# Where the weight rows lie in a partition: a row step of 576 bytes for the input weights, and the output weights moved to the address residue of the left factors

## The chip, the cores and the metric

The kernel runs on one core of one Trainium2 chip. The metric is device time in microseconds for one launch. Five engines matter here: TensorE (PE in the profile, with its weight loads as PEld), VectorE (DVE), ScalarE (ACT), GpSimd (POOL) and the queue of SyncE (SP), which issues nearly all transfers. All of them work on SBUF, a memory of 128 partitions; "address" below always means a byte offset inside a partition, the same for all partitions.

## The reference, cut to what matters

One layer over 528 rows (16 learned tokens and 512 inputs) of 2048 numbers:

```python
hn = _rmsnorm(h_res, norm_in_g[l])
P = hn @ w_in[l]                       # 2048 -> 8320 columns
...                                     # RWKV-7 recurrence on one half, gated short convolution on the other
mix = jnp.concatenate([y_a, y_b], axis=-1)
h_res = h_res + mix @ w_out[l]         # 2048 -> 2048
out = _rmsnorm(h_res, norm_f_g)[:, N_META:]
```

The result has to be accurate to fp32, so each product of two matrices is made of three: a number is split into a high part that the fast fp32 mode of TensorE (fp32r) holds exactly and a low part, and high times high, high times low and low times high are added up.

## The kernel before, in words

**Input projection.** The 8320 output columns are 65 tiles of 128 columns ("lora", and eight each of k, r, v, g, B, C, h and gc). One tile needs 16 blocks of 128 weight rows, and for each block the three products. The weights are the stationary operand of the matmul (TensorE loads 128x128 of them for each one), the normalised rows `xh`/`xl` stream past as the moving operand, in pieces of 264 columns (k, v, lora; two pieces), 258 and 256 (r, g, C, h) or 512 (B, gc). `steps` (line 305) issues these matmuls: 5472 in all. Its inner order is: high weights with `xh`, high weights with `xl`, low weights with `xh`, then the next block.

**How weights come in.** `prefetch` (line 128) loads half a tile (128x1024) into a raw buffer; `split_w` (line 121) cuts it into two quarters of 128x512 and writes the high part with ACT (line 124) and the low part with DVE or POOL (line 125). A quarter holds four blocks side by side, 512 bytes each. There are six buffers for high and six for low quarters. The first four tiles come in smaller pieces (`split_piece`, line 210).

**What sets the order.** PE's order is written out by hand: `fill` and `until` put the projection's matmuls between those of the recurrence. DVE, ACT and POOL are ordered by priorities, by hand in a few stretches. SP's queue is in order: a transfer that waits for a buffer holds the ones behind it.

**Output projection.** From 855 us on. Here the roles are turned: the left factors (`parts`, or the sums `sform` named S1, S3, S4, S5) are stationary and the output weights stream, 512 columns at a time. `product` (line 1213) issues 12 matmuls for a unit; there are 56 units (seven products of a Strassen-like scheme, four quarters of the inner dimension, two halves of the columns). `split_unit` (line 1184) splits output weights into the same twelve buffers as above, or, for the last four units, into the place of old left factors ("home", line 1281). Raw output weights come through `request`, `begin_chain` and `add_by_transfer`; the chain tiles `x..0` to `x..3` hold running sums of them. DVE adds finished products onto the residual rows (`onto`, line 1199), which `load_xa` (line 1262) and `load_xb` bring in; a list of calls by unit number (`at`, line 1259) sets when each is issued.

**Addresses.** A memory pool is a contiguous range of a partition, and its tiles lie one after the other, each rounded up to 32 bytes. In the program before, the twelve quarter buffers (2048 bytes each) start at 4128, the raw buffers follow, then at 40992 `xh`, `xl`, `rs`, `la`, `ones`, `omm`, `hv`, `smask` (pool `xp`), and from 118112 the small pool `tp` (`warm`, three buffers `tm` of 2304 bytes at 118144, 120448 and 122752, `var0`, two `pr`, `b0`, `cv`). After the input projection, `xp` and `tp` are closed and the pool `pw` takes their place from 40992: `ssq`, `fv`, sixteen S tiles of 4096 bytes, `xa0` to `xa3`, chain tile `x03` (at 123072 to 127168), `sh`, `sqj`. A tile of `pw` waits for the tiles that lay in its place (`reuse_waits="tile"`), and for no other.

Taken modulo 512 this means: every block of input weights, high or low, starts at 32. Row kt of `xh` and `xl` starts at 32 + 64 kt, since a row of x is 528 x 4 = 2112 bytes. All left factors start at 192, all output weights at 32, the home tiles at 192. "Distance" below is the address of the weights that are being loaded minus the address of the rows that stream meanwhile, modulo 512. In the input projection of before it goes down by 64 from one block to the next, so each tile goes through eight distances, or sixteen with both pieces of 264. In the output projection it is 192 - 32 = 160, and 0 for the four home units.

Of the kernel before, what the change touches and what calls it, by code (L numbers as in the profile page):

```python
# [18 lines left out]
P = 128  # L19
DM = 2048  # L20
KT = DM // P
SEQ = 512
META = 16
L = SEQ + META
CH = 64
NCH = SEQ // CH + 1
# [20 lines left out]


AHEAD, WEIGHTS = 6000, 3000


def _constants():
# [24 lines left out]
def hymba_kernel(ctx: ExitStack, tc: tile.TileContext, xt, xtok, front, w_in, w_out, pv, lup, cst, msk, gf, out):  # L77
    nc = tc.nc
# [3 lines left out]
    wp = ctx.enter_context(tc.tile_pool(name="wp", bufs=3))  # L82
# [22 lines left out]
    plan = [("lora", 0), ("k", 0), ("r", 0), ("B", 0), ("v", 0), ("k", 1), ("r", 1), ("v", 1), ("g", 0), ("g", 1)]  # L105
# [10 lines left out]
    N_IN = len(stream)  # L116
    stream += [w_out[0, g] for g in range(3)]
    quarters, chain, low = {}, {}, {}
    state = {"next": 0}

    def split_w(q, rq, eng):
        hi = wp.tile([P, 512], F32R, tag="hi", name=f"wh{q}", bufs=6)
        lo = wp.tile([P, 512], F32R, tag="lo", name=f"wl{q}", bufs=6)
        nc.scalar.copy(hi, rq)  # L124
        low[q] = eng.tensor_tensor(out=lo, in0=rq, in1=hi.bitcast(F32), op=ALU.subtract).ins  # L125
        quarters[q] = (hi, lo)
# [13 lines left out]
    cq = ph2.enter_context(tc.tile_pool(name="cq", bufs=1, side="right", reuse_waits="tile"))  # L140
    ph1 = ExitStack()
    xp = ph1.enter_context(tc.tile_pool(name="xp", bufs=1))
    xh = xp.tile([P, KT, L], F32R, name="xh")
    xl = xp.tile([P, KT, L], F32R, name="xl")
    rs = xp.tile([P, L], F32, name="rs")
    la = xp.tile([P, 2, L], F32R, name="la")
    ones = xp.tile([P, P + 2], F32R, name="ones")
    omm = xp.tile([P, 33], F32, name="omm")
    hv = xp.tile([P, 6, 8], F32, name="hv")
    hl = cp.tile([P, 2, 8], F32, name="hl")  # L150
    smask = xp.tile([P, NCH, CH], F32, name="smask")
# [6 lines left out]
    tp = ph1.enter_context(tc.tile_pool(name="tp", bufs=1))  # L158
# [49 lines left out]
        return t  # L208

    def split_piece(n, a, t):  # L210
        hi, lo = quarters[2 * n]
        cols = slice(a, a + t.shape[1])
        nc.scalar.copy(hi[:, cols], t)
        nc.vector.tensor_tensor(out=lo[:, cols], in0=t, in1=hi[:, cols].bitcast(F32), op=ALU.subtract)


    for n in range(4):
        quarters[2 * n] = tuple(
            wp.tile([P, 512], F32R, tag=tag, name=f"w{tag[0]}{2 * n}", bufs=6) for tag in ("hi", "lo")
        )  # L220
# [84 lines left out]
    def steps(ps, ranges, k4, q, ks=range(4), rs_=range(2)):  # L305
        hi, lo = quarters[q]
        for r, (a, b) in enumerate(ranges):
            if r not in rs_:
                continue
            for k in ks:  # L310
                kt = 4 * k4 + k
                w = slice(k * P, (k + 1) * P)
                for n, (ww, xx) in enumerate(((hi, xh), (hi, xl), (lo, xh))):
                    nc.tensor.matmul(  # L314
                        ps[r], ww[:, w], xx[:, kt, a:b], start=(kt == 0 and n == 0), stop=(kt == KT - 1 and n == 2)
                    )
                    yield (b - a) * 0.43

# [14 lines left out]
            nc.vector.tensor_tensor(out=dst[:, a - base : b - base], in0=p, in1=rs[:, a:b], op=ALU.mult)  # L333

    def shift_full(ps, m, name, dst):
        pr = tp.tile([P, L + 1], F32, tag="pr", name=f"pr_{name}", bufs=2)
        nc.gpsimd.memset(pr[:, 0:1], 0.0)
        scaled(FULL, ps, pr, -1)
        sh = tm(f"sh_{name}")[:, 0:L]
        nc.scalar.activation(sh, pr[:, 0:L], AF.Copy, scale=col(V_MU, m))  # L340
        for (a, b), d in dst:
            nc.vector.scalar_tensor_tensor(
                out=d, in0=pr[:, a + 1 : b + 1], scalar=omm[:, m : m + 1], in1=sh[:, a:b], op0=ALU.mult, op1=ALU.add
            )

    def shift_real(ps, m, name, dst):
        pr = tp.tile([P, L + 1], F32, tag="pr", name=f"pr_{name}", bufs=2)
# [112 lines left out]
    def mains():  # L460
        pa = banks(FULL, "lora", pm, "main")
        pb = banks(FULL, "k0", pz, "tz")
        pc = banks(TAIL, "r0", pm, "main")
        pd = [pi.tile([P, SEQ], F32, tag="ser", name="ps_B0")]
        four = ((pa, FULL), (pb, FULL), (pc, TAIL), (pd, REAL))
        for k in range(4):
            for n, (ps, rg) in enumerate(four):
                if k == n == 0:
                    hi, lo = quarters[0]
                    for ww, xx, first in ((hi, xh, True), (lo, xh, False), (hi, xl, False)):  # L470
                        for p, (a, b) in zip(ps, rg):
                            nc.tensor.matmul(p, ww[:, 0:P], xx[:, 0, a:b], start=first, stop=False)
                            yield (b - a) * 0.43
                    continue
                yield from steps(ps, rg, 0, 2 * n, (k,))
        for k4 in range(1, 4):
            for n, (ps, rg) in enumerate(four):
                h = 4 * (k4 // 2) + n
                if k4 == 2:
                    prefetch(h + 3)  # L480
                if (k4, n) == (3, 2):
                    yb = token_scale_sums()
                if (k4, n) == (3, 3):
                    yield from steps(ps, rg, k4, 2 * h + k4 % 2, range(2))
                    token_scale(yb, 4)
                    use("lora", 0, pa)
                    use("k", 0, pb)
                    yield from steps(ps, rg, k4, 2 * h + k4 % 2, range(2, 4))
                    continue
                for r in range(2 if n < 3 else 1):  # L490
                    if (k4, n, r) == (3, 2, 1):
                        token_scale(yb, 0)
                    yield from steps(ps, rg, k4, 2 * h + k4 % 2, range(4), (r,))
        use("r", 0, pc)
        use("B", 0, pd)
        for j in range(4, len(plan)):
# [100 lines left out]
    def behind(dst, src):  # L597
        with tc.issue_after(state["dma"]):
            nc.sync.dma_start(dst, src)
# [450 lines left out]
    pp = ctx.enter_context(tc.tile_pool(name="pp", bufs=1, side="right", reuse_waits="tile"))  # L1050
# [73 lines left out]
    pw = ctx.enter_context(tc.tile_pool(name="pw", bufs=1, reuse_waits="tile"))  # L1124
    po = ctx.enter_context(tc.tile_pool(name="po", bufs=8, space=PSUM, reuse_waits="tile"))
    ssq = pw.tile([P, 4, 5], F32, name="ssq")
    fv = pw.tile([P, 4, 3], F32, name="fv")
    sform = {
        (f, q): [pw.tile([P, 4, HT], F32R, tag=f"{f}{q}{a}", name=f"{f}{q}{a}") for a in range(2)]
        for q in range(2) for f in forms  # L1130
    }
    xa = [pw.tile([P, 1024], F32, name=f"xa{t}") for t in range(4)]

    def split_form(f, q):
        k, tk = forms[f]
# [13 lines left out]
    U = {unit: u for u, unit in enumerate(units)}  # L1149
# [34 lines left out]
    def split_unit(unit, t, home=None):  # L1184
        for q in range(2):
            rq = t()[:, q * 512 : (q + 1) * 512]
            if home is None:
                hi = wp.tile([P, 512], F32R, tag="hi", name=f"oh{U[unit]}{q}", bufs=6)
                lo = wp.tile([P, 512], F32R, tag="lo", name=f"ol{U[unit]}{q}", bufs=6)
            else:  # L1190
                hi, lo = home[q]
            nc.scalar.copy(hi, rq)
            nc.vector.tensor_tensor(out=lo, in0=rq, in1=hi.bitcast(F32), op=ALU.subtract)  # L1193
            right[unit, q] = (hi, lo)
# [64 lines left out]
    def at(u, fn, *args):  # L1259
        calls.setdefault(max(u, -1), []).append((fn, args))  # L1260

    def load_xa(t):
        behind(xa[t], xtok[t * P : (t + 1) * P, 0:1024])

    xb, gfs = [], []
# [32 lines left out]
    for half in range(2):  # L1298
        o = 28 * half
# [28 lines left out]
            at(n + 1, sums, 1)  # L1328
        at(6 + n, split_form, f, 1)
    for t in range(4):  # L1330
        at((0, 1, 8, 9)[t], load_xa, t)
    at(13, load_gain)
    for m in range(2):
        at(21 + m, load_xb, m)
# [161 lines left out]
```

## Time and profile before

| | |
|---|---|
| median of 3 runs | 1025.31 us (1024.43 to 1025.73) |
| span of the profiled execution, first to last instruction | 1023.6 us |
| TensorE busy, share of the span | 1006.6 us, 98% |
| VectorE / ScalarE / GpSimd busy | 686.1 / 393.8 / 273.8 us |
| granted TensorE clock, mean | 0.996 |

The profiled execution's own time is not given apart from its span; the median stands 1.7 us above the span. Times inside the run are microseconds from its first instruction. Matmuls are pipelined: a row's duration runs from its start to its modelled end and overlaps the next one, so the pace of TensorE is read from start to start, or from a piece of the chain of waits, which counts each stretch of time once.

### The profile page before, as it was taken

What the parts mean: (1) busy time and instruction counts of PE and PEld (TensorE: products, weight loads), DVE (VectorE), ACT (ScalarE), POOL (GpSimd) and SP (SyncE); (2) the same over time, 40 slices, a digit from 0 to 9 for tenths busy, and PEclk for the clock granted to TensorE, in tenths of its full rate; (3) what the DMA queues carried; (4) which work ended last, traced back from release to release, by engine and by line L of the source; (5) the groups of instructions that cost most, each with busy time, mean ns of one, the idle gap of its engine ahead of it and who ended that gap; (6) DMA issues with size and microseconds to landing.
All of it is one profiled execution on the core that took longest, in us unless ns stands there. A gap on an engine that the chain in (4) does not pass through costs nothing.

```text
span 1023.6 us, 23708 instructions
## 1 busy us (share of the span) xinstructions
PE 1006.6 (98%) x9723; PEld 919.0 (90%) x9723; DVE 686.1 (67%) x1239; ACT 393.8 (38%) x729; POOL 273.8 (27%) x292
## 2 busy tenths in 40 slices
PE   9999999999999999999999999999999999999996
PEld 8899998999988999998999998889889897787885
DVE  7677954587765569654669653244555697998787
ACT  7553423344313434322434322222222335445453
POOL 0122323233332323232322232123332332015001
PEclk9999999999999999999999999999999999999999
DMA  9526476546764364864263845867673688695754
GB/s 333 152 63 148 122 190 182 150 123 143 167 172 134 96 170 99 217 167 117 83 166 98 220 139 168 309 212 235 195 232 93 183 276 192 172 319 135 172 125 165
DMA packets 185036, 174.82 MB, mean 171 GB/s; under 512 B 121568, under 2 KB 142816, under 8 KB 184416
## 3 DMA queue, kind: packets, MB, share of 16 engines
q1 hardware_dynamic: 182336, 164.40, 55.8%
q0 software_dynamic: 2304, 8.39, 4.7%
q8 instruction: 76, 1.25, 0.5%
q10 hardware_dynamic: 288, 0.52, 0.1%
q14 instruction: 32, 0.26, 0.1%
HBM read 136.92 MB, written 36.35 MB: 169 GB/s over the span
## 4 chain that ended last, share of the span: by engine, by line
PE 68%; DVE 8%; DMA 4%; issue 2%; SPq 1%; ACT 1%; POOL 0%; DVEq 0%; ACTq 0%; POOLq 0%
PE ps_gc L314 8%; PE ps_h L314 8%; PE ps_B L314 7%; PE ps_k L314 7%; PE ps_v L314 7%; PE ps_C L314 7%; PE ps_g L314 7%; PE ps_r L314 7%; DVE ol L1193 3%; DMA wo<-in_w_out_dram 2%; PE M L1220 2%; PE g L659 1%; PE zs L984 1%; PE Q L1220 1%; DVE xb L1201 1%
## 5 line engine op out<-in xcount | busy, mean ns | idle before, releaser
L125 POOL TENSOR_TENSOR wl<-wr,wh 128x512 fp32r<-128x512 f32 x119 | 169.2, 1423 | 370.8 <-ACT wh L124 356.4
L124 ACT CAST wh<-wr 128x512 fp32r<-128x512 f32 x252 | 152.7, 618 | 294.8 <-PE ps_C L314 51.9
L125 DVE TENSOR_TENSOR wl<-wr,wh 128x512 fp32r<-128x512 f32 x133 | 100.9, 765 | 109.0 <-ACT wh L124 108.6
L314 PE MATMUL ps_k<-xh,wl 128*128 128x264 f32 x256 | 73.1, 286 | 1.1 <-DVE wl L125 1.1
L314 PE MATMUL ps_v<-xh,wh 128*128 128x264 f32 x256 | 73.0, 285 | 0.0
L314 PE MATMUL ps_h<-xh,wh 128*128 128x258 f32 (+1 forms) x256 | 72.8, 284 | 0.0
L314 PE MATMUL ps_k<-xh,wh 128*128 128x264 f32 x256 | 72.8, 284 | 0.0
L314 PE MATMUL ps_v<-xl,wh 128*128 128x264 f32 x256 | 72.7, 284 | 0.0
L314 PE MATMUL ps_v<-xh,wl 128*128 128x264 f32 x256 | 72.7, 284 | 0.0
L314 PE MATMUL ps_k<-xl,wh 128*128 128x264 f32 x256 | 72.6, 284 | 0.0
L314 PE MATMUL ps_C<-xh,wh 128*128 128x258 f32 (+1 forms) x256 | 72.6, 284 | 0.0
L314 PE MATMUL ps_h<-xh,wl 128*128 128x258 f32 (+1 forms) x256 | 72.3, 282 | 0.2 <-issue 0.2
L314 PE MATMUL ps_r<-xh,wh 128*128 128x258 f32 (+1 forms) x256 | 72.4, 283 | 0.0
L314 PE MATMUL ps_g<-xl,wh 128*128 128x258 f32 (+1 forms) x256 | 72.3, 282 | 0.0
L314 PE MATMUL ps_r<-xl,wh 128*128 128x258 f32 (+1 forms) x256 | 72.2, 282 | 0.0
L314 PE MATMUL ps_g<-xh,wl 128*128 128x258 f32 (+1 forms) x256 | 72.0, 281 | 0.0
L314 PE MATMUL ps_C<-xl,wh 128*128 128x258 f32 (+1 forms) x256 | 72.0, 281 | 0.0
L314 PE MATMUL ps_g<-xh,wh 128*128 128x258 f32 (+1 forms) x256 | 72.0, 281 | 0.0
L314 PE MATMUL ps_h<-xl,wh 128*128 128x258 f32 (+1 forms) x256 | 71.9, 281 | 0.0
L314 PE MATMUL ps_r<-xh,wl 128*128 128x258 f32 (+1 forms) x256 | 71.9, 281 | 0.0
L314 PE MATMUL ps_C<-xh,wl 128*128 128x258 f32 (+1 forms) x256 | 71.9, 281 | 0.0
L314 PE MATMUL ps_B<-xh,wl 128*128 128x512 f32 x128 | 51.3, 401 | 0.0
(353 smaller groups left out, 3006.2 us busy)
## 6 DMA issues: line engine op xcount, KB each, us to landing
wr<-in_w_in_dram SPq DMA_DIRECT2D x126, 512.0 KB
ct<-opd SPq DMA_DIRECT2D x64, 288.0 KB
wo<-in_w_out_dram SPq DMA_DIRECT2D x24, 512.0 KB
x<-in_w_out_dram POOLq DMA_DIRECT2D x16, 512.0 KB, 6.2
opd<-ar SPq DMA_DIRECT2D x8, 576.0 KB
opd<-gt SPq DMA_DIRECT2D x16, 288.0 KB
opd<-bt SPq DMA_DIRECT2D x64, 64.0 KB
x<-in_w_out_dram SPq DMA_DIRECT2D x8, 512.0 KB
```

The lines of the kernel that those rows point to most:

```text
L124: nc.scalar.copy(hi, rq)
L125: low[q] = eng.tensor_tensor(out=lo, in0=rq, in1=hi.bitcast(F32), op=ALU.subtract).ins
L314: nc.tensor.matmul(ps[r], ww[:, w], xx[:, kt, a:b], start=(kt == 0 and n == 0), stop=(kt == KT - 1 and n == 2))
L659: nc.tensor.matmul(z[h][:, c - c0], bk[hs, c, h : h + 2, :].rearrange("p a s -> p (a s)"), ar[hs, c].rearrange("p a s -> p (a s)"), start= ...
L984: nc.tensor.matmul(d[hs, j], w, x[hs], start=(a == 0), stop=(a == b - 1))
L1193: nc.vector.tensor_tensor(out=lo, in0=rq, in1=hi.bitcast(F32), op=ALU.subtract)
L1201: nc.vector.tensor_tensor(out=h, in0=h, in1=ps, op=op)
L1220: nc.tensor.matmul(bank[s], left(prod, jj, m, s), w, start=(jj == 0 and n == 0), stop=(jj == 7 and n == 2))
```

## The change

Each of the twelve quarter buffers grows from 512 to 688 numbers (2752 bytes), as a tag of its own that is used in turn. Inside it, a quarter of input weights is no longer 4 x 512 bytes in a row: its four blocks start 576 bytes apart (64 modulo 512, as rows of x do). The start inside the buffer is chosen so that all blocks of a half tile have the same distance to their rows of x, and each of the sixteen halves of one kind of tile (e = 2 i + half) another, in steps of 32. Output weights stay contiguous, and start where they have the residue 192 of the left factors.

The buffers take 8448 bytes more. To make room, `la`, `ones`, `omm`, `hv`, `smask` and the two `pr` tiles move to the pool `cq` on the other side of the memory, and only two of the four `xa` tiles stay in `pw`; `xa2` and `xa3` go into the place of `mix1` (tag R1), and their loads are issued at units 10 and 11 instead of 8 and 9. `fv` is padded from 12 to 80 numbers, which puts the S tiles at 192 again.

```diff
+WSLOT, WSTEP = 688, 144
+WFIRST, XROWS, LEFTS = 32, 288, 192
...
+    def pair(name):
+        slot = made[0] % 6
+        made[0] += 1
+        return [
+            (
+                wp.tile([P, WSLOT], F32R, tag=f"{tag}{slot}", name=f"{name[0]}{tag[0]}{name[1:]}", bufs=1),
+                4 * WSLOT * (2 * slot + n),
+            )
+            for n, tag in enumerate(("hi", "lo"))
+        ]
+
+    def by_rows(q):
+        j = q // 2
+        tile_n, half = (j % 4, j // 4) if j < 8 else (j // 2, j % 2)
+        what, i = plan[tile_n]
+        e = 0 if what == "lora" else 2 * i + half
+        goal = XROWS - 32 * e + 256 * (q % 2)
+        return [
+            bass.AP(tensor=t.tensor, offset=t.offset + o, ap=[list(t.ap[0]), [WSTEP, 4], [1, P]])
+            for t, at in pair(f"w{q}")
+            for o in [(goal - WFIRST - at) % 512 // 4]
+        ]
+
+    def in_line(name):
+        return [
+            t[:, o : o + 512] for t, at in pair(name) for o in [(LEFTS - WFIRST - at) % 512 // 4]
+        ]
+
     def split_w(q, rq, eng):
-        hi = wp.tile([P, 512], F32R, tag="hi", name=f"wh{q}", bufs=6)
-        lo = wp.tile([P, 512], F32R, tag="lo", name=f"wl{q}", bufs=6)
+        if q < 2 * N_IN:
+            hi, lo = by_rows(q)
+            rq = rq.rearrange("p (k c) -> p k c", c=P)
+        else:
+            hi, lo = in_line(f"w{q}")
...
-    la = xp.tile([P, 2, L], F32R, name="la")
+    la = cq.tile([P, 2, L], F32R, name="la")
...
-        pr = tp.tile([P, L + 1], F32, tag="pr", name=f"pr_{name}", bufs=2)
+        pr = cq.tile([P, L + 1], F32, tag="pr", name=f"pr_{name}", bufs=2)
...
-                        ps[r], ww[:, w], xx[:, kt, a:b], start=(kt == 0 and n == 0), stop=(kt == KT - 1 and n == 2)
+                        ps[r], ww[:, k], xx[:, kt, a:b], start=(kt == 0 and n == 0), stop=(kt == KT - 1 and n == 2)
...
-    fv = pw.tile([P, 4, 3], F32, name="fv")
+    fv = pw.tile([P, 4, 20], F32, name="fv")
...
-    xa = [pw.tile([P, 1024], F32, name=f"xa{t}") for t in range(4)]
+    xa = [pw.tile([P, 1024], F32, name=f"xa{t}") for t in range(2)]
...
-                hi = wp.tile([P, 512], F32R, tag="hi", name=f"oh{U[unit]}{q}", bufs=6)
-                lo = wp.tile([P, 512], F32R, tag="lo", name=f"ol{U[unit]}{q}", bufs=6)
+                hi, lo = in_line(f"o{U[unit]}{q}")
...
     def load_xa(t):
+        if t == 2:
+            later_rows = pp.tile([P, 2, 1024], F32, tag="R1", name="xa2")
+            xa.extend(later_rows[:, n] for n in range(2))
...
-        at((0, 1, 8, 9)[t], load_xa, t)
+        at((0, 1, 10, 11)[t], load_xa, t)
```

More of the change, by code (lines that the diff above doesn't have):

```diff
@@ L119, in hymba_kernel @@
     state = {"next": 0}
-    def split_w(q, rq, eng):
-        hi = wp.tile([P, 512], F32R, tag="hi", name=f"wh{q}", bufs=6)
-        lo = wp.tile([P, 512], F32R, tag="lo", name=f"wl{q}", bufs=6)
+    made = [0]
+    def pair(name):
[23 more added lines that the diff above has]
+        ]
+    def split_w(q, rq, eng):
+        if q < 2 * N_IN:
[3 more added lines that the diff above has]
+            hi, lo = in_line(f"w{q}")
         nc.scalar.copy(hi, rq)
@@ L145, in hymba_kernel @@
     rs = xp.tile([P, L], F32, name="rs")
-    la = xp.tile([P, 2, L], F32R, name="la")
-    ones = xp.tile([P, P + 2], F32R, name="ones")
-    omm = xp.tile([P, 33], F32, name="omm")
-    hv = xp.tile([P, 6, 8], F32, name="hv")
+    la = cq.tile([P, 2, L], F32R, name="la")
+    ones = cq.tile([P, P + 2], F32R, name="ones")
+    omm = cq.tile([P, 33], F32, name="omm")
+    hv = cq.tile([P, 6, 8], F32, name="hv")
     hl = cp.tile([P, 2, 8], F32, name="hl")
-    smask = xp.tile([P, NCH, CH], F32, name="smask")
+    smask = cq.tile([P, NCH, CH], F32, name="smask")
     pm = ph1.enter_context(tc.tile_pool(name="pm", bufs=4, space=PSUM))
@@ L210, in split_piece @@
     def split_piece(n, a, t):
[L211 to L214, printed above, removed]
+        ks = slice(a // P, (a + t.shape[1]) // P)
+        hi, lo = (w[:, ks] for w in quarters[2 * n])
+        t = t.rearrange("p (k c) -> p k c", c=P)
+        nc.scalar.copy(hi, t)
+        nc.vector.tensor_tensor(out=lo, in0=t, in1=hi.bitcast(F32), op=ALU.subtract)
     for n in range(4):
-        quarters[2 * n] = tuple(
-            wp.tile([P, 512], F32R, tag=tag, name=f"w{tag[0]}{2 * n}", bufs=6) for tag in ("hi", "lo")
-        )
+        quarters[2 * n] = by_rows(2 * n)
     F0, F1, F2 = KT + P + L, 4 * P + L, 8 * P + 2 * L
@@ L311, in steps @@
                 kt = 4 * k4 + k
-                w = slice(k * P, (k + 1) * P)
                 for n, (ww, xx) in enumerate(((hi, xh), (hi, xl), (lo, xh))):
                     nc.tensor.matmul(
-                        ps[r], ww[:, w], xx[:, kt, a:b], start=(kt == 0 and n == 0), stop=(kt == KT - 1 and n == 2)
+                        ps[r], ww[:, k], xx[:, kt, a:b], start=(kt == 0 and n == 0), stop=(kt == KT - 1 and n == 2)
                     )
@@ L346, in shift_real @@
     def shift_real(ps, m, name, dst):
-        pr = tp.tile([P, L + 1], F32, tag="pr", name=f"pr_{name}", bufs=2)
+        pr = cq.tile([P, L + 1], F32, tag="pr", name=f"pr_{name}", bufs=2)
         scaled(TAIL, ps, pr, 14)
@@ L471, in mains @@
                         for p, (a, b) in zip(ps, rg):
-                            nc.tensor.matmul(p, ww[:, 0:P], xx[:, 0, a:b], start=first, stop=False)
+                            nc.tensor.matmul(p, ww[:, 0], xx[:, 0, a:b], start=first, stop=False)
                             yield (b - a) * 0.43
```

## The prediction, made before the changed kernel was run

> **What bounds the kernel now.** I read the page's head first, then the chain of waits, then the list of what TensorE waited for, and last the timeline and the windows for the few places where something else comes close.
>
> ```profile
> span 1023.6 us, 23708 instructions
> PE 1006.6 (98%) x9723; PEld 919.0 (90%) x9723; DVE 686.1 (67%) x1239; ACT 393.8 (38%) x729; POOL 273.8 (27%) x292
> PEclk9999999999999999999999999999999999999999
> ...
> PE 68%; DVE 8%; DMA 4%; issue 2%; SPq 1%; ACT 1%; POOL 0%; DVEq 0%; ACTq 0%; POOLq 0%
> ```
> ```profile
> PE t L831 <- DVE xn L822: 2.2, 1, 2.2
> PE prs L454 <- POOL yb L447: 1.7, 1, 1.7
> PE pwarm L173 <- DVE cold L170: 1.4, 1, 1.4
> PE ps_k L314 <- DVE wl L125: 1.1, 1, 1.1
> PE M L1220 <- DVE ol L1193: 1.0, 3, 0.5
> PE Q L1220 <- DVE ol L1193: 0.6, 1, 0.6
> ```
>
> TensorE is busy nearly always, its clock is full, and these waits, its longest, come to 8.0 us. So the time is the number of matmuls times their pace, and an address change acts through the pace. The pace, from pieces of the chain of waits (start, length, how many):
>
> ```profile
> 479.68 11.65 PE ps_k L314 x96
> 821.54 11.41 PE ps_h L314 x96
> 832.95 11.11 PE ps_B L314 x48
> 893.56 5.60 PE M L1220 x24
> ```
>
> That is 121.4 ns for a matmul of 264 columns, 118.9 for 258 and 256, 231.5 for 512 in the input projection, and 233.3 for 512 in the output projection. The two paces of 512 columns differ though shapes, engine and clock are the same; what differs is the address distance: it steps through 0, 64, ... in the first, and stays at 160 in the second. The home units at the end, at distance 0, are a third case (timeline):
>
> ```profile
> 1003.84 5.63 PE L1220 MATMUL end<-home,m 128*128 128x512 f32 x24
> 1009.31 5.91 PE L1422 MATMUL end<-home,m 128*128 128x256 f32 x48
> ```
>
> The 24 start within 1009.31 - 1003.84 = 5.47 us: 227.9 ns each, 5.4 ns less than at 160. So distance does matter, by a few per cent at most. The same trace has odd against even multiples of 32: in a k tile, twelve matmuls on the first piece (even) alternate with twelve on the second (odd). Starts of the runs:
>
> ```profile
> 479.51 0.28 PE L314 MATMUL ps_k<-xh,wh 128*128 128x264 f32 x1
> ...
> 480.96 0.29 PE L314 MATMUL ps_k<-xh,wh 128*128 128x264 f32 x1
> ...
> 482.43 0.28 PE L314 MATMUL ps_k<-xh,wh 128*128 128x264 f32 x1
> ...
> 483.88 0.28 PE L314 MATMUL ps_k<-xh,wh 128*128 128x264 f32 x1
> ...
> 485.34 0.28 PE L314 MATMUL ps_k<-xh,wh 128*128 128x264 f32 x1
> ```
>
> Even: 1.45 + 1.45 = 2.90; odd: 1.47 + 1.46 = 2.93. Odd costs 0.03 us per 24, or 1.2 ns per matmul (a difference of the size of the rows' rounding, so weak).
>
> **The change, term by term.**
>
> *Input projection, 5472 matmuls.* Before, each tile steps through all distances; after, each half tile keeps one, and the halves of a kind step through all sixteen. So every distance gets the same share as before, with one exception: pieces of 512 and 256 columns had only even multiples of 32 and now have odd ones in half of their tiles. For 256: 1536 / 2 x 1.2 ns = 0.9 us. For 512 I use 160, the only odd multiple seen: 768 / 2 x (233.3 - 231.5) = 0.7 us. Pieces of 264 had both kinds and keep both; pieces of 258 start 56 bytes further on, which no row separates: 0. Term: +1.6 us. What no row shows is whether a distance that stays has the same price as one met in passing. Two places with a constant distance exist: 160 is dearer than the passing mean (233.3 against 231.5), 0 is cheaper (227.9). If all halves settle like 160, this is 1.8 x 768 = 1.4 us, and with 256 and 258 at the steady home pace ((5.91 - 0.28) / 47 = 119.8 ns against 118.9) another 0.9 x 3072 = 2.8 us: +4.2 in all; with 264 columns off by as much as 512 at 160 (0.8% of 1632 x 121.4 ns) +1.6 more. If all settle like 0: (231.5 - 227.9) x 768 = 2.8 us less, and with 264 at the same 1.6% 3.2 us less. Ends -6.0 and +5.8. I take +1.6, since the trace is nearest to an even mix.
>
> A rule stands against any effect: the Trainium skill's page "SBUF — State Buffer", section "Who interferes with whom", gives TensorE one read port for the moving operand and an independent one for the weight load, and says that it never waits on anyone. By it this term and the next would be 0. The rows above (227.9 against 233.3 ns) do not agree with it.
>
> *Output weights at distance 0.* The 52 units ahead of the home ones go from 160 to 0: 12 x 5.4 = 65 ns a unit, 3.4 us as seen from TensorE. How much arrives? Windows of 10 us (PE, PEld, DVE, ACT, POOL busy, clock, DMA share, GB/s):
>
> ```profile
> 875.00:885.00 10.00, 9.44 (x40) 7.01 (x39) 10.00 (x14) 4.13 (x8) 0.87 (x1) 1.00 0.61 135
> 925.00:935.00 10.00, 10.00 (x45) 8.04 (x44) 7.53 (x9) 5.20 (x11) 4.48 (x3) 1.00 0.55 157
> 985.00:995.00 10.00, 10.00 (x45) 8.04 (x44) 10.00 (x18) 7.31 (x14) 0.88 (x1) 1.00 0.50 108
> 995.00:1005.00 10.00, 10.00 (x44) 7.78 (x43) 10.00 (x18) 2.35 (x5) 0.00 (x0) 1.00 0.02 4
> ```
>
> DVE has no idle time near 880, where TensorE already waits for it (the `ol` rows above, 1.6 us), nor from 985 to 1005. There a faster TensorE only meets low parts (`ol`) that are not ready: those are late next. Only the stretch between, from about 885 to 943, is paced by TensorE: some 20 units, 1.3 us, less 0.3 for its end, where two of the `ol` waits lie. I take -1.0; ends -3.4 and 0.
>
> *Splitting into rows 576 bytes apart.* Same instruction counts. Existing instructions with separate rows:
>
> ```profile
> L1138 ACT CAST S<-mix x8: 1042/1047/1055, 858.7 to 872.9; 128x1024 fp32r<-128x1024 f32 x8
> L1139 DVE TENSOR_TENSOR S<-mix,S x8: 1218/1224/1234, 860.7 to 887.4; 128x1024 fp32r<-128x1024 f32 x8
> ...
> L124 ACT CAST wh<-wr 128x512 fp32r<-128x512 f32 x252 | 152.7, 618 | 294.8 <-PE ps_C L314 51.9
> L125 POOL TENSOR_TENSOR wl<-wr,wh 128x512 fp32r<-128x512 f32 x119 | 169.2, 1423 | 370.8 <-ACT wh L124 356.4
> ...
> 879.29 1.23 DVE L1182 TENSOR_TENSOR wo<-wo,wo 128x1024 f32<-128x1024 f32 x1
> ```
>
> The S tiles are read in four separate rows: ACT takes 1047 against 618 ns for half as many contiguous numbers (0.84 ns per extra number), DVE 1224 ns against 1.23 us for the contiguous add. So separate rows are free on the reading side; written rows are not seen, and I take the same. POOL has no such row; it idles 371 us before its splits, and TensorE waited for a split 1.1 us in all. Price 0; ends 0 and +1, since without that cover a slower POOL would show as a wait on `wl`.
>
> *Moved tiles.* `xa2`/`xa3` now wait for the last reader of `mix1`, the S split at 887.4 + 1.2 = 888.6. SP holds behind them only what follows:
>
> ```profile
> 885.27 8.44 SPq L1173 DMA_DIRECT2D wo<-in_w_out_dram  x2
> ```
>
> Two requests, the second at 885.27 + 8.44 - 0.33 = 893.4, so 888.6 delays nothing; the rows are first added after unit 16 (about 904). Cost 0. The tiles sent to `cq` add no instruction; what the recurrence loads in their place was last used long before. Cost 0, at most the 0.4 us that TensorE already waits there.
>
> The smaller `pw` is another matter: the buffers end 8448 bytes higher, `fv` takes 256 more (48 to 320, rounded), two `xa` tiles are gone, so chain tile `x03` lies at 123584 to 127680. `tp` starts at 119136, its `tm` buffers at 119168, 121472 and 123776. `x03` therefore overlaps the last 192 bytes of the second and all of the third; before, it touched the third alone.
>
> ```profile
> 845.68 1.75 POOL L420 TENSOR_TENSOR cv<-cv,b 128x512 f32<-128x512 f32 x1
> 847.46 0.33 SPq L1169 DMA_DIRECT2D x<-in_w_out_dram  x1
> 856.61 0.69 DVE L361 SCALAR_TENSOR_TENSOR gc<-th_c,gc 128x512 f32<-128x512 f32 x1
> 861.52 2.17 ACT L1192 CAST oh<-x 128x512 fp32r<-128x512 f32 x4
> 862.94 2.49 DVE L1193 TENSOR_TENSOR ol<-x,oh 128x512 fp32r<-128x512 f32 x4
> 929.40 4.16 DMA wo<-in_w_out_dram
> ```
>
> Before, its load was issued at 847.46, as POOL's last read of `b7` ended (845.68 + 1.75). The second buffer holds `th_c7`, read until 856.61 + 0.69 = 857.3. So the load goes out 10 us later, and behind it on SP the `xa0`/`xa1` loads. A load of its size takes about 4.2 us (929.40), which gives 861.5, just when ACT wants it (861.52); busy engines can add 2. Behind ACT's cast stand DVE's first `ol` pair and unit 3 on TensorE. I take +0.5; ends 0 and +3.
>
> *Sum:* +1.6 - 1.0 + 0.5 = +1.1 us on the span of 1023.6, so 1024.7; on the median, which stands 1.7 above the span, 1026.4.
>
> **The rivals.**
>
> *Constant distances settle at the dear prices* (slower). For it: 160 and the home pace of 256 columns, two of three steady paces, lie above the passing ones. Against: 0 lies below. Price +4.2 in place of +1.6, or +5.8 with 264: 1029 to 1030.6. It decides once more than about half of the sixteen distances behave like 160.
>
> *They settle at the cheap prices* (faster). For it: 227.9 at 0. It takes -6.0 at most; half of it, -3, with -1.0 and +0.5 gives 1022; the whole gives 1019. Against: no other distance is seen at that price.
>
> *Chain tile 3 is late* (slower): the load takes 7 us instead of 4.2, +3 at unit 3: 1029. Against: SP's queue is empty then.
>
> *Distance does nothing*, as in the skill's rule: 1025.3 + 0.5 = 1025.8. Against: 5.4 ns between 160 and 0; only other work at the end could explain it.
>
> **How the numbers follow.** About 0.2% (2 us) is what a measurement of this kernel can tell from no change. Forecast 1026.4 with 0.34 (its own range 1024 to 1029); dear distances 0.31; cheap ones 0.20; late chain tile 0.07; no effect of distance 0.08. Faster (below 1023.3): the cheap case and 0.03 of the forecast, 0.23. Same (to 1027.4): 0.25 of the forecast and the no-effect case, 0.33. Slower: dear, late and 0.06 of the forecast, 0.44. The range goes from the cheap case short of its end, 1020.5, to the dear one with the late tile, 1031.5.
>
> **What would show it.** In the chain of waits, pieces of 48 matmuls of one B or gc tile should spread by tile (each half its own pace) around 231.5 ns, not keep one; units of the output projection should fall from 2.80 to about 2.73 us, with new waits on `ol` after 985; the load of `x03` should be issued at about 857.3. The prediction is wrong if the tiles' mean pace moves by more than 0.5%, if units stay at 2.80, or if TensorE stops for hi or lo at 863 for over 2 us.

## The result, and the profile after

| | before | after |
|---|---|---|
| median of 14 runs each | 1025.41 us | 1027.57 us (1025.85 to 1030.04) |
| ratio, 95% interval | | 1.0023 (1.0015 to 1.0031) |
| span of the profiled execution | 1023.6 us | 1026.3 us |

The change costs 2.2 us. The head of the profile after, and its chain of waits by engine:

```profile
span 1026.3 us, 23702 instructions
PE 1006.2 (98%) x9723; PEld 920.9 (90%) x9723; DVE 688.7 (67%) x1239; ACT 393.7 (38%) x729; POOL 272.2 (27%) x292
...
PE 83%; DVE 8%; DMA 4%; issue 2%; ACT 1%; SPq 1%; POOL 0%; DVEq 0%; ACTq 0%; POOLq 0%
```

TensorE is as busy as before (1006.2 against 1006.6 us), though each unit of the output projection became shorter. What TensorE waited for (total us, times, longest):

```profile
PE t L866 <- DVE xn L857: 2.3, 1, 2.3
PE prs L489 <- POOL yb L482: 1.7, 1, 1.7
PE M L1254 <- ACT oh L1226: 1.6, 1, 1.6
PE M L1254 <- DVE ol L1227: 1.5, 4, 0.7
...
PE Q L1254 <- DVE ol L1227: 0.6, 1, 0.6
PE zy L1023 <- issue: 0.5, 1, 0.5
```

New are the 1.6 us on `oh`, a high part that ACT had not made in time, and 0.5 us more on `ol` in the M units. Pieces of the chain (start, length, how many), the last tiles of the projection, the chain tile and two units:

```profile
801.54 11.16 PE ps_gc L349 x48
812.71 11.44 PE ps_C L349 x96
824.14 11.43 PE ps_h L349 x96
835.57 11.14 PE ps_B L349 x48
846.71 11.15 PE ps_gc L349 x48
...
860.03 6.78 DMA x<-in_w_out_dram
...
897.93 5.44 PE M L1254 x24
```

Each projection tile is 0.01 to 0.04 us longer than the same tile before (11.12, 11.41, 11.41, 11.11 and 11.14). The units went from 2.80 to 5.44 / 2 = 2.72 us, as they should at distance 0. The DMA row is chain tile 3, 6.78 us on the path. Its neighbours in the timeline:

```profile
860.03 0.33 SPq L1204 DMA_DIRECT2D x<-in_w_out_dram  x1
...
866.91 2.18 ACT L1226 CAST oh<-x 128x512 fp32r<-128x512 f32 x4 [2.63 <-DMA x<-in_w_out_dram]
```

It is issued 12.6 us later than before (847.46), and ACT stands still for 2.63 us until it lands.

I summed the time from each matmul's start to the next one's, by line (5466 matmuls of the projection, 648 of the output units; home's second half is 5.63 us in every run). The projection went from 756.15 to 758.01 us, the output units only from 154.28 to 154.08: 52 units x 80 ns = 4.2 us were won, and all but 0.2 us of it was lost again in longer units. The rest (recurrence, +1.0 us) is for one half a stop on issue, a time in which TensorE waits for nothing that the profile shows; such stops come and go between kernels that are equal there, and I take nothing from them.

All kernels together (medians in us; the ratio is to the kernel before on the same chip; the two sums are of one profiled execution each, and stops on issue move the projection's by up to about 1 us). An interval is 0.8 to 1.6 us wide to either side, so steps of about 1 us between two rows are not clear of nothing by the medians alone; what the traces show then has to carry the reading.

```
                 median   ratio, 95% interval       projection  output units
after            1027.57  1.0023 [1.0015, 1.0031]   758.01      154.08
e1_out_only      1024.55  0.9992 [0.9981, 1.0003]   756.58      153.17
e2_chain3        1026.40  1.0013 [1.0004, 1.0022]   758.01      153.51
e3_dear          1032.25  1.0065 [1.0049, 1.0081]   763.29      155.71
e4_cheap         1025.37  1.0004 [0.9994, 1.0013]   754.90      154.97
e5_step512       1026.38  1.0011 [1.0002, 1.0020]   756.90      153.98
e6_hilo          1026.00  1.0007 [0.9998, 1.0016]   757.40      154.35
e7_gains         1024.01  0.9983 [0.9974, 0.9993]   759.19      149.64
e8_cheap3        1021.62  0.9967 [0.9954, 0.9979]   754.83      151.75
e9_all           1018.39  0.9924 [0.9910, 0.9937]   753.97      149.95
e10_out160       1029.13  1.0032 [1.0020, 1.0045]   758.26      156.08
e11_before_gains 1024.21  0.9995 [0.9986, 1.0004]   756.56      153.03
e12_out_gains    1021.13  0.9966 [0.9955, 0.9976]   756.16      150.26
```

### The profile page after: what moved, and what is told of

Same layout as the page of the kernel before. It is cut to its first block, busy times and chain, and to the rows that moved or that the text cites. A ratio compares the mean times of both kernels' runs of the same rounds, so it can differ in the third digit from the quotient of the medians.

```text
span 1026.3 us, 23702 instructions
## 1 busy us (share of the span) xinstructions
PE 1006.2 (98%) x9723; PEld 920.9 (90%) x9723; DVE 688.7 (67%) x1239; ACT 393.7 (38%) x729; POOL 272.2 (27%) x292
## 3 DMA queue, kind: packets, MB, share of 16 engines
q8 instruction: 76, 1.25, 0.5%
## 4 chain that ended last, share of the span: by engine, by line
PE 83%; DVE 8%; DMA 4%; issue 2%; ACT 1%; SPq 1%; POOL 0%; DVEq 0%; ACTq 0%; POOLq 0%
PE ps_k L349 9%; PE ps_v L349 9%; PE ps_g L349 9%; PE ps_h L349 9%; PE ps_r L349 9%; PE ps_B L349 9%; PE ps_gc L349 8%; PE ps_C L349 8%; DVE ol L1227 3%; DMA wo<-in_w_out_dram 2%; PE g L694 2%; PE M L1254 2%; PE ps_lora L349 1%; PE zs L1019 1%; PE zy L1023 1%
## 5 line engine op out<-in xcount | busy, mean ns | idle before, releaser
L162 POOL TENSOR_TENSOR wl<-wr,wh 128x512 fp32r<-128x512 f32 x119 | 167.5, 1408 | 372.7 <-ACT wh L161 361.8
```

## The experiments

**Output weights at distance 0, alone** (on the kernel before):

```diff
-    mhalf = cp.tile([P, 8], F32, name="mhalf")
+    mhalf = cp.tile([P, 48], F32, name="mhalf")
-    fv = pw.tile([P, 4, 3], F32, name="fv")
+    fv = pw.tile([P, 4, 26], F32, name="fv")
```

> The kernel before with one thing of the change alone: the small pool with mhalf is 160 bytes longer and fv is padded, so that all quarter buffers and the rows of x move together by 160 bytes. The input projection keeps its distances; the output weights come to distance 0 from the left factors, and chain tile 3 lies as in the kernel before. Theory 1 (distance sets the pace, and the late chain tile 3 eats the gain in the full change): units of the output projection fall from 2800 to about 2720 ns, 52 x 80 = 4.2 us as TensorE would have it alone, of which DVE's stretches near 870 and 985 to 1005 take back 60 to 75%: 1.0 to 1.8 us faster than before, about 1024. Rival (DVE hides all of it): no change, 1025.4, with units at 2720 but longer waits on the low parts. Rival (nothing is lost): 1021.2. Rival (distance does not set the pace): units stay at 2800.

Measured: 0.7 us below before, less than the 1.0 to 1.8 that was expected, with an interval that just takes in no change. All units that wait for nothing take 2720 ns, so distance does set the pace; what arrives is about a sixth of it. The converse, the changed kernel with the output at 160 again:

```diff
-WFIRST, XROWS, LEFTS = 32, 288, 192
+WFIRST, XROWS, LEFTS = 32, 288, 32
```

> The changed kernel with the output weights back at residue 32, distance 160 from the left factors; the rest as changed. Units of the output projection should take 2800 ns again. Theory 1 (DVE takes back most of the faster pace): 0.7 to 1.5 us slower than the changed kernel, 1028.3 to 1029, since its stops for chain tile 3 and on the low parts shrink. Rival (the whole 52 x 80 ns counts): 1031.7. Rival (nothing arrives): 1027.5.

Units are back at 2800 ns, the sum of the output units rises by 2.0 us, the time by 1.6. Both runs point the same way, 0.7 and 1.6 of 4.2 us, but neither is clear of the rival that nothing arrives; that the whole 4.2 us arrive is out in both.

**Chain tile 3 in time** (on the changed kernel):

```diff
-    xa = [pw.tile([P, 1024], F32, name=f"xa{t}") for t in range(2)]
+    xa = [pw.tile([P, 1024 + 48 * t], F32, name=f"xa{t}")[:, 0:1024] for t in range(2)]
```

> The changed kernel with xa1 48 numbers longer, so that chain tile 3 starts at 123776 and no longer covers the last 192 bytes of the second tm buffer; nothing else moves. Theory 1 (its late load, at 860.0 in place of 847.5, makes TensorE stop in units 2 and 3, about 2.1 us): the load goes out near 850, TensorE does not stop for hi and lo near 863 to 868, and the kernel is 1 to 2 us faster than the changed one, about 1026. Rival (the late tile is hidden, the loss is elsewhere, in the input projection or in DVE's work): 1027.5 with the load near 850 all the same.

Measured: 1.2 us less than the changed kernel. The same two instructions in its timeline, of which ACT's now waits for nothing:

```profile
849.97 0.33 SPq L1204 DMA_DIRECT2D x<-in_w_out_dram  x1
...
864.11 2.17 ACT L1226 CAST oh<-x 128x512 fp32r<-128x512 f32 x4
```

Units 2 and 3 fell from 4442 and 3381 to 2720 and 3120 ns, 2.0 us, but the sum of all units fell by only 0.6: the units at 874 and 878 stayed as they were, and those at 936 to 943 (0.5 us longer) and from 984 on (1.0 us) took the rest in this profile. So the late tile costs about 1.2 us in the time here, not the 2 us that are seen at it. That is no fixed price: of the two kernels with cheap distances, e4_cheap and e8_cheap3 in the table, the second has the tile in time and is 3.8 us faster (1021.62 against 1025.37), with output units 3.2 us shorter in sum; the distances of k and v, in which the two differ as well, account for about 1 us of it by the triples below.

**The same distance in all halves of a kind.** For each kind of tile the distance that the changed kernel's trace was read to show as the dearest, and then the cheapest:

```diff
-        e = 0 if what == "lora" else 2 * i + half
+        e = 0 if what == "lora" else {"k": 12, "v": 12, "B": 9, "gc": 9}.get(what, 3)
```
```diff
-        e = 0 if what == "lora" else 2 * i + half
+        e = 0 if what == "lora" else {"k": 15, "v": 15, "B": 0, "gc": 0}.get(what, 8)
```

> The changed kernel, but each kind of tile keeps one distance in all its halves, the dearest that the changed kernel's trace shows for its width: 160 for B and gc (512 columns), 160/128 for k and v (264), 360/352 for r, g, C and h (258 and 256). Theory 1 (the price of a distance belongs to the distance, and adds up): 256 triples of 512 columns x (701.9 - 696.3 ns) = 1.4 us, r, g, C, h 2.3 us, k and v 0.9 us: 4.6 us slower than the changed kernel, about 1032.2. Rival (the spread between tiles is of their neighbours or their place in the run, not of distance): 1027.5.

> The changed kernel, but each kind of tile keeps one distance in all its halves, the cheapest that the changed kernel's trace shows: 448 for B and gc (691.2 ns a triple against a mean of 696.3), 200/192 for r, g, C and h (348.2 for 256 columns against 353.9), 32/0 for k and v. Theory 1: 1.3 us for 512 columns, 2.9 us for r, g, C and h, 0.7 us for k and v, 4.9 us faster than the changed kernel, about 1022.7. Rival (the spread is of the tiles, not of distance): 1027.5. If the dear kernel is slower and this one is not faster, a gain of pace is lost elsewhere (splits that are not ready), and new waits of TensorE on the weights will show it.

For k and v the 12 of the first edit gives 128 on the first piece and 96 on the second, not the 160 and 128 that the expectation names. The dear one came out at 1032.25, where the sum of prices put it. The cheap one gained 2.2 of 4.9 us. The same tiles in the chain of the dear kernel:

```profile
804.83 11.22 PE ps_gc L349 x48
816.05 11.50 PE ps_C L349 x96
...
839.08 11.22 PE ps_B L349 x48
```

and of the cheap one:

```profile
430.76 11.20 PE ps_C L349 x96
...
798.94 11.07 PE ps_gc L349 x48
810.01 11.37 PE ps_C L349 x96
...
832.74 11.07 PE ps_B L349 x48
```

B and gc differ by 0.15 us a tile (1.4%), C by 0.13. The two kernels issue the same instructions on the same data, differ by multiples of 32 bytes in where input weights lie, and are 6.9 us apart. The Trainium skill's page "SBUF — State Buffer", section "Who interferes with whom", says that TensorE's two read ports are independent; these two runs do not agree with it.

Two parts of the cheap one's forecast failed. Three matmuls on one piece (a triple; counted from the first start to the start of the next matmul on that piece, without those in which TensorE stopped) cost, in ns: 512 columns 692.9 (forecast 691.2) and 256 columns 349.0 (348.2) held; but k and v cost 367.3 where 364 to 365 was expected. The choice was not borne out by the trace that it came from: the two halves that have this pair of distances (32 and 0) stood at 366.0 there, above the mean of 365.8, and the cheapest pair of that trace was 0 and 480 with 363.6, of only 18 triples. Second, a distance has not one price. Tile C took 11.20 us at 431 and 11.37 at 810, with the same distance: triples of 256 columns average 342 ns in the stretches of 400 to 450 and 550 to 600 us, and 347 to 353 in the others. What puts a whole tile into the one or the other stays open.

**The old distances in the new buffers:**

```diff
-WSLOT, WSTEP = 688, 144
+WSLOT, WSTEP = 688, 128
-        goal = XROWS - 32 * e + 256 * (q % 2)
+        goal = XROWS
```

> The changed kernel with the four blocks of a quarter of input weights in a row again (WSTEP 128, every block at residue 288, that of the first row of x): all buffers, moved tiles, chain tile 3 and the output weights at distance 0 stay as in the changed kernel, and the projection goes through the eight or sixteen distances as in the kernel before. Theory 1 (constant distances cost the 1.9 us by which the projection's matmuls grew, 756.15 to 758.01 us): 1.9 us faster than the changed kernel, about 1025.7; the projection is back at 756.2, units of the output stay at 2720 ns, TensorE still stops for hi and lo of chain tile 3. Rival (the 1.9 us come from other buffers or are chance): 1027.5.

1.2 us less than the changed kernel, where 1.9 was expected. The triples of 512 and 264 columns, by distance, have the prices of the kernel before though every address moved (512 columns at 0: 690.1 and 690.1 ns; at 256: 690.5 and 690.5; 264 columns at 256: 359.3 and 359.4; at 416: 369.0 and 368.0). Those of 256 columns do not at one distance (64: 347.3 and 352.9), nor those of 258 (136: 363.6 and 360.7), so distance is not all that counts. By these runs the projection's loss is of the distances, and it is 1.1 to 1.9 us.

**Which load counts?**

```diff
-        e = 0 if what == "lora" else 2 * i + half
-        goal = XROWS - 32 * e + 256 * (q % 2)
+        wide = what in ("k", "v", "lora")
+        goals = [XROWS - 32 * e + 256 * (q % 2) for e in ((2, 0) if wide else (0, 14))]
-            for t, at in pair(f"w{q}")
+            for goal, (t, at) in zip(goals, pair(f"w{q}"))
```

> The changed kernel with another distance for high and low weights: B, gc, r, g, C and h have high weights 64 below the row of x (448) and low ones level with it (0), in all halves; k, v and lora likewise on their first piece. The sequence of a block is high, high, low; while a row streams, the weights of a later matmul are loaded. Theory A (the load of the next matmul counts): the distances met are 448, 0, 0, and B and gc take about 690 ns a triple. Theory B (the load after the next counts): all are 0, as in the output projection, and B and gc take 680 ns a triple in place of 696.3, 256 x 16 ns = 4.2 us for these two alone, about 1023. Rival C (the distance of a tile as a whole does it): as in the cheap kernel at 448 or the changed one at 0, 691 to 696 ns, 1026 to 1027.

B and gc took 695.8 ns a triple: A and B are both out, and C holds only as "no gain". k, v and lora fell to 362.3 ns, below all that a single held distance gave them (held: the same for all blocks of a half tile, where the kernel before meets each distance only in passing), while 258 columns rose from 358.9 to 362.0. Tile B by form, duration min/median/max in ns, in this kernel:

```profile
L349 PE MATMUL ps_B<-xh,wh x64: 387/396/502, 658.1 to 844.5; 128*128 128x512 f32 x64
L349 PE MATMUL ps_B<-xl,wh x64: 389/397/497, 658.3 to 844.7; 128*128 128x512 f32 x64
L349 PE MATMUL ps_B<-xh,wl x64: 387/393/497, 658.5 to 845.0; 128*128 128x512 f32 x64
```

and in the cheap one:

```profile
L349 PE MATMUL ps_B<-xh,wh x64: 388/393/502, 657.5 to 843.0; 128*128 128x512 f32 x64
L349 PE MATMUL ps_B<-xl,wh x64: 387/388/496, 657.8 to 843.2; 128*128 128x512 f32 x64
L349 PE MATMUL ps_B<-xh,wl x64: 389/396/505, 658.0 to 843.4; 128*128 128x512 f32 x64
```

In each, one product of the three is the cheap one: high weights with `xl` in the cheap kernel, low weights with `xh` here. By these medians the price is made matmul by matmul, and neither rule that I tried says by which pair of addresses. That stays open.

**Why so little of the output's gain arrives.** Eight products with the final norm's gain run on POOL at 919 to 945 us. The kernel with the output change alone, in its timeline (start, length, engine):

```profile
919.62 4.69 DVE L1201 TENSOR_TENSOR xa<-xa,sh 128x512 f32<-128x512 f32 x4
919.68 1.77 POOL L1278 TENSOR_TENSOR xa<-xa,gfb 128x512 f32<-128x512 f32 x1 [11.71 <-ACT sqj_None L1207]
921.76 1.39 POOL L1278 TENSOR_TENSOR xa<-xa,gfb 128x512 f32<-128x512 f32 x1 [0.31 <-ACT sqj_None L1207]
...
937.13 1.28 POOL L1278 TENSOR_TENSOR xa<-xa,gfb 128x512 f32<-128x512 f32 x1 [0.20 <-ACT sqj_None L1207]
...
937.58 1.38 DVE L1193 TENSOR_TENSOR ol<-x,oh 128x512 fp32r<-128x512 f32 x1 [0.76 <-ACT oh L1192]
```

DVE's `ol` takes 0.69 us alone; here it starts during POOL's product and ends 0.55 us after that product does (938.96 against 938.41), as if it had waited for its end. The same holds in all seven places where DVE started such an operation during one of the eight products: each ended 0.55 to 0.56 us after the product, and together they took 7.1 us more than alone. The same section of the Trainium skill has a DVE instruction with two SBUF inputs contend with a GpSimd one that reads SBUF, and calls the ports that they share an exclusive lock; the trace agrees. So I moved the eight to DVE, into a stretch where it waits for transfers:

```diff
+    def late_gain(t, n):
+        with tc.issue_after(state["low"]):   # the last low part issued on DVE
+            gain(t, n, nc.vector)
...
-        at(30 + 2 * n, gain, n // 2, n % 2, nc.gpsimd)
+        at(36 + n, late_gain, n // 2, n % 2)
```

First on the changed kernel with chain tile 3 in time:

> The kernel with xa1 longer (chain tile 3 in time), and the eight products with the final norm's gain that POOL does between 921 and 947 moved to DVE, behind the low parts of units 38 to 45 (about 950 to 985), where DVE waits for transfers. In the trace DVE's operations take about twice as long while POOL multiplies (4.68 us for 4 instead of 1.29 for 2), and units at 936 to 946 take 3296, 3237 and 3340 ns in place of 2720, 1.7 us in all. Theory 1 (the gain of the output's pace is lost to DVE): these three units come to 2720, and 0.5 to 1.7 us of it arrives: 1024.7 to 1025.9. Rival (transfers set the end from 950 on, so what is won at 940 is lost again at 985): the units are at 2720, and the time stays at 1026.4, with longer units from 984 on.

2.4 us less than without it, more than Theory 1 allowed, because the longer units at 985 to 1002 went too: behind 890 us only one unit is not 2720 ns. The rival (transfers set the end) is out. Another rival is that POOL also issues the transfers that add to the chain tiles, and that products which stand ahead of these transfers held them up. In the kernel with the output change alone three of the four such transfers at 936 to 945 us went out after POOL had sat idle for 1.0 to 3.1 us until DVE's `ol`; only the fourth (944.62) stood directly behind a product. So it was mainly DVE that held them. Is that a gain of its own, or the output's gain arriving? The same edit on the kernel before, and on the kernel with the output at distance 0:

> The kernel before, with one thing: the eight products with the final norm's gain go from POOL to DVE, behind the low parts of units 38 to 45. The output weights stay at distance 160. In the trace of before, units longer than 2800 ns behind 935 us sum to 0.46 + 0.56 + 0.23 = 1.25 us. Theory 1 (these stops come from POOL's products, which slow DVE): about 1.2 us faster than before, 1024.2. Rival (the products cost as much on DVE): 1025.4.

> The kernel before, with the output weights at distance 0 (as in the run with that alone) and the eight products with the gain on DVE. Theory 1 (the faster pace of the output projection did not arrive because DVE, slowed by POOL's products, could not follow): with both, most of 52 x 80 ns arrives, so this kernel is 3 to 3.6 us faster than the one with the moved products alone, about 1021, though the pace alone gave 0.7 us. Rival (the two gains only add up, 0.7 + 1.2): 1023.5.

Without the faster pace the edit is worth 0.4 us (the interval takes in none), not the 1.2 that was expected, though in its profile the output units did fall by 1.25 us (153.03 against 154.28). With it, the step from distance 160 to 0 is worth 1024.21 - 1021.13 = 3.1 us, in place of 0.7. What DVE waited for from 945 to 1005 us, with the eight on POOL (output change alone):

```profile
DVE wo L1182 <- DMA wo<-in_w_out_dram: 6.8, 3, 2.9
DVE home L1193 <- ACT home L1192: 3.4, 1, 3.4
DVE ol L1193 <- ACT oh L1192: 0.8, 1, 0.8
```

and with them moved:

```profile
DVE ol L1193 <- ACT oh L1192: 2.6, 3, 1.3
DVE wo L1182 <- DMA wo<-in_w_out_dram: 2.0, 3, 1.3
DVE home L1193 <- ACT home L1192: 1.3, 1, 1.3
```

The chain of waits tells the order. With the eight on POOL it leaves TensorE at 912 us, runs through DVE's instructions, among them those that were held up beside the products, and then goes round: DVE's parts free a raw buffer, a transfer fills it, DVE takes it up.

```profile
910.15 2.05 PE Q L1220 x9
912.23 0.64 ACT oh L1192
...
948.58 3.65 DMA wo<-in_w_out_dram
...
958.38 3.63 DMA wo<-in_w_out_dram
...
968.23 4.96 DMA wo<-in_w_out_dram
...
976.95 6.40 DMA wo<-in_w_out_dram
983.38 0.63 ACT home L1192
```

With them moved, the chain stays on TensorE up to 966:

```profile
929.78 14.96 PE M L1220 x66
...
963.78 2.06 PE Q L1220 x9
```

So what DVE lost at 920 to 945 was carried to the end by that ring, and came back as the late parts at 985 to 1005.

**What pays, together.** First the cheap distances (k and v left as changed) with chain tile 3 in time, then all, with the high/low pair for k, v and lora and the moved products:

> The kernel with xa1 longer (chain tile 3 in time) and the cheap distances for B and gc (448) and r, g, C, h (200/192), while k and v keep one distance for each half, as in the changed kernel. Theory 1 (prices add up): from 1026.4, 512 triples of 256 columns x (353.9 - 349.0) = 2.5 us, 256 of 512 x (696.3 - 692.9) = 0.9, 512 of 258 x 0.3 = 0.15: 3.5 us less, 1022.9, faster than the kernel before by 2.4 us. Rival (what the projection wins is lost in the output projection, where splits and transfers set the time): 1024 to 1025, with output units longer than in the kernel with chain tile 3 alone.

> All that paid, in one kernel: xa1 longer (chain tile 3 in time), the eight products with the final norm's gain on DVE behind units 38 to 45, and for each kind the distances that measured cheapest: 448 for B and gc (693.0 ns a triple), 200/192 for r, g, C and h (358.7 and 349.1), and for k, v and lora the pair with high weights 64 below the low ones (362.3 against 365.5). If the prices add up: 1021.6 (distances and chain tile 3) less 512 x 3.2 ns = 1.6 us for k and v, less the 2.4 us of the moved products: 1017.6. Rival (DVE or a transfer takes back what the products won once TensorE comes 4 us earlier): 1019 to 1020.

1021.62 and 1018.39. The first gained more than its forecast (1022.9), the second 0.8 us less (1017.6). The last is 0.76% faster than before (interval 0.63% to 0.90%); its span and what TensorE still waits for of the output's low parts:

```profile
core 0 of [0], span 1017.6 us
...
PE M L1254 <- DVE ol L1227: 0.7, 1, 0.7
...
PE Q L1254 <- DVE ol L1227: 0.6, 1, 0.6
```

## Why the prediction was right or wrong, by its steps

The time came out 1.2 us above the forecast and inside the forecast's own range. The three terms that count were +1.6, -1.0 and +0.5, and measured as follows.

- **Input projection, +1.6: near in the sum, wrong in its split.** The profile's sum rose by 1.9 us, undoing it gave 1.2. By triples: 256 columns 512 x (353.92 - 353.06) = 0.4 us (forecast 0.9), 512 columns 0.0 (0.7), 258 columns 0.2 (0), 264 columns 544 x (365.78 - 365.06) = 0.4 (0); 1.1 us in all. That odd multiples of 32 are dearer was right on the mean: held, the odd ones cost 698.3 and the even ones 694.4 ns at 512 columns, and 355.2 against 352.8 at 256. The step that failed is that the even ones keep the price that they have in passing and the odd ones lie above it by the price of 160. At 512 columns the eight distances cost 695.5 on the mean in passing; the odd ones lie 2.8 ns above that (forecast 5.4) and the even ones, held, 1.1 below. Single ones moved more: in the kernel before, 0 costs 690.1 and 256 costs 690.5, held they cost 696.2 and 695.0. Triples of 512 columns in the changed kernel:

```
distance     0     32    64    96    128   160   192   224
ns         696.2 701.6 694.0 695.3 696.5 701.9 692.7 694.7
distance   256    288   320   352    384   416   448   480
ns         695.0 701.5 695.1 695.7 694.8 700.6 691.2 695.0
```

  Every fourth step (32, 160, 288, 416) is dear, the other odd ones are not, and the mean, 696.3, is that of the passing distances (696.1). The choice that decided, an even mix, came out: neither the dear nor the cheap rival came about, since the halves step through all sixteen. That the mean of the held prices comes so near to that of the passing ones was partly luck, since single distances moved by up to 6 ns. That dear and cheap held distances both exist is shown by the kernels with one distance each.
- **Constant 0 is not what it is at home.** A half of an input tile at 0 costs 696.2, not 3 x 227.9. There, unlike here, the weights of the next block do not lie 64 further on; that this is the reason was not settled (the kernel with high and low weights apart).
- **Output weights, -1.0: right in size (0.7 alone, 1.6 when undone, as far as the intervals tell), and the place (new waits on `ol`), but not for the reason given.** A unit gained 80 ns, where the prediction had 65. I took DVE's lack of idle time at 985 to 1005 as a bound of its own. It is the end of a ring that POOL's products at 919 to 945 start; with these moved, 3.1 us arrive. The stretch that I called paced by TensorE, up to 943, holds the cause, so the size came right in part by luck.
- **Chain tile 3, +0.5: the mechanism was right, the size was not; it is about 1.2 us.** The issue came at 860.03 (857.3, plus the 2.7 us by which all was later by then). The load took 6.78 us, not 4.2 plus 2, and the units at 863 and 867 became 2.1 us longer than before: the sign that I had named as making the prediction wrong, and the rival of a late chain tile with its 7 us. In this kernel its price of 3 us at unit 3 was too high, since later stops of TensorE grew when this one went.
- **Splits into separate rows, 0: right.** ACT and POOL in the changed kernel:

```profile
L161 ACT CAST wh<-wr 128x512 fp32r<-128x512 f32 x252 | 152.8, 618 | 298.2 <-PE ps_C L349 48.3
L162 POOL TENSOR_TENSOR wl<-wr,wh 128x512 fp32r<-128x512 f32 x119 | 167.5, 1408 | 372.7 <-ACT wh L161 361.8
```

  618 ns as before, and 1408 against 1423.
- **Moved `xa2`/`xa3` and the `cq` tiles, 0: right in price, not in time.** The queue waited for the last S split and issued the two loads at 893.43, not at 888.6, for which the prediction had this split end (its 893.4 is another request's, so that the numbers agree is chance):

```profile
SPq L634 <- DVE S L1174: 3.2, 1, 3.2
```

  That they cost nothing shows in TensorE's waits, none of which is on them. The rows that wait on `ct` still show 0.4 us.
- **Distance does nothing: out**, by the dear and cheap kernels.

The terms as measured, 1.1 to 1.9, less 0.7 to 1.6, plus 1.2, give 0.7 to 2.4 and so hold the 2.2 us, though each is about as large as its uncertainty. Of the 1.2 us by which the forecast fell short the late tile accounts for 0.7; where the rest lies stays open.

## What to carry to other kernels

When two operands of one engine meet in a memory, measure the price of their distance per instruction shape before rearranging: here a mix of distances cost about the same as before, a distance that is held did not have the price that it has in passing, and only picking one for each shape by measurement paid. A new address map also moves tile overlaps, and one that reaches 192 bytes into its neighbour's life cost about as much as the distances did; list the overlaps before and after. When an engine "has no idle time" where a gain gets lost, follow the chain of waits backwards through buffers and transfers to the point where it leaves the bounding engine: the cause lay 40 us and more earlier, in another engine's instructions.

## What the runs showed of the hardware that I had not expected

- Where weights lie relative to the streamed rows, in steps of 32 bytes, moves matmuls of 512 columns between 691 and 702 ns a triple, and the whole kernel between 1025.4 and 1032.3 us.
- Held or met in passing, one distance has two prices: at 512 columns 0 costs 696.2 ns a triple held and 690.1 in passing; at 264 columns 256 costs 365.7 and 359.3.
- At one and the same distance, tiles of 256 columns ran at 342 ns a triple in some stretches and at 347 to 353 in others. High weights 64 bytes below the low ones gave 264 columns 362.3 ns, less than any single held distance (364.0 to 368.2).
- A product on POOL of 1.3 to 1.8 us holds up a DVE operation with two SBUF inputs to its own end: seven such operations each ended 0.55 to 0.56 us after the product, 0.7 to 1.4 us later than they would alone. Four of DVE's took 4.69 us beside two products, and 2.49 us once these were moved.
